# One decoder layer on one Trainium2 core: the FFN mean's factor moved in the order of the gate and up products, two weight sums moved to VectorE, one sum and one cast moved at the end

## The chip, the core and the metric

The kernel runs on 1 core of one Trainium2 chip. The core has a matrix engine (TensorE: PE, with its weight loads shown as PEld), three engines for everything else (VectorE: DVE; ScalarE: ACT; GpSimd: POOL), and SyncE (SP), which here issues most of the DMA transfers; POOL issues some too. The engines run side by side, each works through its own queue in order, and semaphores hold an instruction back until its inputs are there and its output buffer is free. Operands lie in SBUF (128 partitions); matmuls write PSUM, which has eight banks of 128 x 512 float32.

The metric is device time in microseconds (us) for one execution of the whole layer; lower is better. A profiled execution has besides a span, from its first to its last instruction.

## The reference

One layer of a hybrid decoder on 512 tokens of width 1024. It has a mixer (stick-breaking attention and a gated convolution), a cross-attention into 256 memory tokens, and a SwiGLU feed-forward part, each behind an RMS norm and followed by a residual add. The change is in the feed-forward part, cut here to what matters:

```python
def rms_norm(x, g):
    var = jnp.mean(xf * xf, axis=-1, keepdims=True)
    return xf * lax.rsqrt(var + EPS) * g
...
hf = rms_norm(x, norm_ffn[l])
gate, up = jnp.split(hf @ w_ffn_in[l], 2, axis=-1)        # 1024 x 2816 each
x = x + (jax.nn.silu(gate) * up) @ w_ffn_out[l]           # 2816 x 1024
```

The factor rsqrt(var + EPS) is one number per token. It can be multiplied in after the products, and the kernel does so.

## The kernel before

**Stages.** The mixer runs to about 346 us of the span, the cross-attention to about 502 us, the gate and up products to about 724 us, and the down projection with the final norm to the end. Activations are held transposed: features on partitions, tokens along the row. Every float32 operand is split into a rounded part (hi, cast by ACT) and a remainder (lo, a subtraction on DVE at L996 or alike), and each product is three matmuls: hi x hi, hi x lo, lo x hi.

**Gate and up products.** The 2816 hidden columns are 22 slices m of 128 (`NF` = 22). For a slice, gate and up over a pair of input blocks form a 2x2 block product, which is computed with seven products instead of eight (a Winograd form). So a slice needs seven products i = 0 to 6, each over four pairs of input blocks (`product`, L899). They add into three PSUM banks: `z` (i = 0, 3, 4, 5, one after the other), `v` (i = 1) and `y` (i = 2, then 6). After products 0, 3 and 4 ACT copies `z` away (`reads`, L935: tiles `sa`, `sb`); the next product into `z` cannot start before that copy is done. DVE adds the two halves of `v` after product 1 and of `y` after product 6 (L932 and L933), and of `y` once more before product 6 (`second`, L946); product 6 waits for the latter, because it overwrites the bank.

**Weights of a slice.** `ffn_load(m)` (L844) fetches two tiles, `wg` and `ws` (`s13`), with SP, and adds a third piece into `ws` with an accumulating transfer issued by POOL; `load_corner(m)` (L862) fetches `a`. Two sums then finish the seven weight combinations: `sum_third(m)` (L869) adds a half of `ws` into `wg`, and `sum_last(m)` (L873) writes the sum of the two halves of `wg` into `a`. Both are 128x512 additions, on DVE unless an engine is given. `pair_cast(m, which)` (L879) casts `wg`, `ws` or `a` (which = 0, 1, 2), 128x1024, on ACT for products (0, 1), (4, 2) or (5, 6); `third_cast(m)` (L896) casts the weight of product 3. `rest_of` (L995) takes the remainder on DVE. `made(n, cast, ...)` (L1112) queues the cast at place n and the remainder one place later.

**The order.** In this stage the program order of PE, ACT and DVE is written by hand (`manual_schedule`, L1184); SP and POOL, and all other stages, are laid out by a planner that works with the dependencies and estimated costs. The list `uses` (L970) gives the order of the products; n is a place in it:

```python
uses = [(0, 0), (0, 1), (0, 2), (1, 0), (1, 1), (0, 3), (1, 3), (0, 4), (1, 2), (0, 5), (0, 6),
        (1, 4), (2, 0), (2, 1), (1, 5), (1, 6)]
for m in range(2, NF - 1):
    uses += [(m, 3), (m, 2), (m, 4), (m + 1, 0), (m + 1, 1), (m, 5), (m, 6)]
```

so (1, 2) is place 8, and (0, 5), (0, 6) are places 9 and 10. At each n the loop at L1191 issues the product, then its reads, then what `at(n, ...)` has queued there, and last, at two values of n, the parts of the mean. For the last slices the list ends (20, 3), (20, 2), (20, 4), (21, 0), (21, 1), (20, 5), (21, 3), (21, 2), (21, 4), (20, 6), (21, 5), (21, 6). In the code at L1160, n is the place of (20, 5); from there on the first parts of the down projection are fitted in too: `w0` and `w1` are casts of its weights, `x0` to `x3` casts of its activations.

**The mean.** `mean2()` (`squares_mean`, L183) splits the sum of squares `acc` into `acch` and `accl` on DVE; `along` (L205) then multiplies both by a constant matrix on PE, which leaves the mean in the PSUM tile `varb`, and calls `rstd_of` (L118). That takes Ln and Exp on ACT for a first value, and refines it with one Newton step on DVE: `rv` = var + EPS, `ra` = y y, `ra` = -0.5 ra rv, `r0b` = (ra + 1.5) y. `turn_r2` (L980) writes a row of `r0b` to DRAM and reads it back turned, with two transfers of POOL. `evict` (L950) multiplies a slice by `r0b`, takes the SiLU on ACT, and forms the activation. `rstd_of` also serves the mixer's norm, the memory tokens' norm and the norm of the cross-attention.

Of the kernel before, what the change touches and what calls it, by code (L numbers as in the profile page):

```python
# [11 lines left out]
ALU = mybir.AluOpType  # L12
# [32 lines left out]
def hybrid_layer(ctx: ExitStack, tc: tile.TileContext, xT_d, memT_d, mem_d, cols_d, wv_d, win_d,  # L45
# [69 lines left out]
        after(i, [last])  # L115
        return [i]

    def rstd_of(var, n, s, tables=()):  # L118

        def new(t):  # L120
            return tmp(t, n) if n > TT else spool.tile([P, n], F32, tag=t, name=nm(t))

        v, y, a = new("rv"), new("ry"), new("ra")
        r = cpool.tile([P, n], F32, tag=s, name=nm(s))
        after(nc.scalar.activation(y, var, AF.Ln, bias=eps_t), tables)
        nc.vector.tensor_scalar(out=v, in0=var, scalar1=EPS, scalar2=None, op0=ALU.add)
        exps.append(nc.scalar.activation(y, y, AF.Exp, scale=-0.5))
        nc.vector.tensor_tensor(out=a, in0=y, in1=y, op=ALU.mult)
        nc.vector.scalar_tensor_tensor(out=a, in0=a, scalar=-0.5, in1=v, op0=ALU.mult,
                                       op1=ALU.mult)  # L130
        nc.vector.scalar_tensor_tensor(out=r, in0=a, scalar=1.5, in1=y, op0=ALU.add, op1=ALU.mult)
        return r

    def chained(i):

# [47 lines left out]
    def squares_mean(acc, n, folded=False):  # L183

        if folded:
            low, high = HALVES
            t, both = tmp("accf"), unit("acch", n * P)
            nc.scalar.copy(t[low, :], acc[high, :])
            nc.vector.tensor_tensor(out=t[low, :], in0=t[low, :], in1=acc[low, :], op=ALU.add)
            nc.vector.tensor_copy(both[low, :], t[low, :])  # L190
            nc.vector.tensor_tensor(out=both[high, :], in0=t[low, :], in1=f(both[low, :]),
                                    op=ALU.subtract)
            parts = both,
        else:
            parts = unit("acch", n * P), unit("accl", n * P)
            nc.vector.tensor_copy(parts[0], acc)
            nc.vector.tensor_tensor(out=parts[1], in0=acc, in1=f(parts[0]), op=ALU.subtract)

        def mean(bank):
            vp = bank("varb")[:, :n * P]  # L200
            for part in parts:
                nc.tensor.matmul(vp, mean_r, part, start=part is parts[0], stop=part is parts[-1])
            return vp

        def along(s, tables=(), bank=otile):  # L205

            vp = mean(bank)
            return rstd_of(vp, n * P, s, tables)

        def turned(s, tables=(), bank=otile):  # L210

            row = tmp("vrow")
            nc.scalar.copy(row[0:1, :n * P], mean(bank)[0:1, :])
            return rstd_of(turned_row(row[0:1, :n * P], n, "v" + s, nc.sync, nc.sync), n, s, tables)

        return along, turned


# [890 lines left out]
    def at(n, *some):  # L1109
        todo.setdefault(n, []).extend(some)  # L1110

    def made(n, cast, *args, late=1):  # L1112

        parts = []
        at(n, lambda: parts.append(cast(*args)))
        at(n + late, lambda: rest_of(*parts[0]))
# [3 lines left out]
    made(2, pair_cast, 0, 2)  # L1120
    at(3, lambda: load_corner(2))
    made(4, pair_cast, 1, 1)
    made(7, pair_cast, 2, 0)
    made(9, pair_cast, 1, 2)
    at(9, lambda: sum_third(2, nc.gpsimd))
    at(13, lambda: evict(0, 0))
    at(14, lambda: evict(0, 1))
    at(15, lambda: evict(0, 2))
# [2 lines left out]
    for m in range(1, NF - 1):  # L1131
        p = {i: uses.index((m, i)) for i in range(2, 7)}
        q = {i: uses.index((m + 1, i)) for i in range(2)}
        if m > 1:
            at(p[3], lambda m=m: sum_third(m + 1))
            at(p[3], lambda m=m: evict(m - 1, 0))
            at(p[2], lambda m=m: evict(m - 1, 1))
            at(q[0], lambda m=m: evict(m - 1, 2))
            made(p[3], pair_cast, m, 2)
            made(p[2], third_cast, m + 1)  # L1140
        else:
            made(p[4], third_cast, m + 1)
        at(p[4], lambda m=m: second(m))
        if m + 2 < NF:
            at(p[4], lambda m=m: load_corner(m + 2))
        made(q[0], pair_cast, m + 1, 1, late=2)
        at(q[1], lambda m=m: sum_last(m + 1)) if m > 1 else at(11, lambda: sum_last(2, nc.gpsimd))
        if m + 2 < NF:
            made(p[5], pair_cast, m + 2, 0)
    at(uses.index((0, 4)), lambda: second(0))  # L1150
# [7 lines left out]
        return lambda: rest_of(*held.pop(s))  # L1158

    n = uses.index((NF - 2, 5))  # L1160
    made(n, pair_cast, NF - 1, 2)
    at(n, lambda: begun("w0", out_cast, *w01(0))(), begun("x0", cast_first, 0))
    at(n + 1, ended("w0"), ended("x0"), begun("x2", half_form, 2, 0, 0))
    at(n + 2, ended("x2"), lambda: n2_of(halves(acts[0][1])[0], 0), begun("x1", cast_first, 1))
    at(n + 3, lambda: second(NF - 1), ended("x1"), begun("x3", half_form, 3, 0, 0), ended("x3"))
    at(n + 4, lambda: evict(NF - 2, 0), begun("x2", half_form, 2, 1, 0),
       lambda: begun("w1", out_cast, *w01(1))(), lambda: evict(NF - 2, 1), ended("x2"),
# [16 lines left out]
    with tc.manual_schedule(engines={mybir.EngineType.PE, mybir.EngineType.Activation,  # L1184
# [6 lines left out]
        for n, (m, i) in enumerate(uses):  # L1191
# [4 lines left out]
            reads(m, i)  # L1196
            for part in todo.get(n, ()):
                part()
            if n == 8:
                mean2 = mean2()  # L1200
            elif n == 10:
                r2b[0] = mean2[0]("r0b", bank=mmtile)
                turn_r2()

        evict(NF - 1, 1)
# [317 lines left out]
```

## Time and profile before

| what | us |
|---|---|
| time, median of 3 runs | 841.49 |
| lowest and highest run | 841.46 and 842.75 |
| the profiled execution, its time | 841.48 |
| the profiled execution, its span | 839.8 |
| gate and up products, from and to (of the span) | about 502 to 724 |
| busy in that window: PE, DVE, ACT, POOL | 221.13, 208.36, 116.26, 28.18 |

The profile is of one execution. A row of a timeline has the start in us from the span's start, the busy time in us, the engine, the line of the code, the operation, the tile written and the tiles read, shapes, and how many instructions are merged; brackets give the engine's idle time before it and what ended that. Matmuls overlap: their busy times add up to more than the distance of their starts. A row of the waits has the waiting engine, line and tile, what it waited for, and the total in us, the number of times and the longest.

### The profile page before, as it was taken

The numbers are of one execution on the slowest core, as the hardware profiler recorded it, in microseconds if no ns is written. First come the engines' busy times: TensorE is split into PE (matmuls) and PEld (weight loads), VectorE is DVE, ScalarE is ACT, GpSimd is POOL, SyncE is SP. The second block draws the span as 40 slices with busy tenths as digits, with TensorE's granted clock in tenths as the row PEclk, the third lists the DMA queues.
The fourth block names the chain that finished last, engine by engine and source line by source line (L and its number), as shares of the span: only waits on it lengthen the run. The fifth ranks groups of instructions, "written<-read, shape, count | busy, mean of one in ns | idle before, by whom it ended". The sixth has DMA issues, their size and how long they took to land.

```text
span 839.8 us, 12035 instructions
## 1 busy us (share of the span) xinstructions
PE 830.6 (99%) x4430; PEld 716.8 (85%) x4430; DVE 682.0 (81%) x1070; ACT 458.3 (55%) x778; POOL 164.2 (20%) x170
## 2 busy tenths in 40 slices
PE   9999999999999999999999999999999999999996
PEld 7888888888888888888888889999999999888885
DVE  7879899986756577586555689999999999999886
ACT  7567878674332355433444556644455545576654
POOL 0011131110666620173000032111111110000401
PEclk9999999999999999999999999999999999999999
DMA  8553454134687865556421326577767663465552
GB/s 302 153 167 101 121 115 112 61 121 167 235 314 274 314 230 199 188 229 235 151 75 51 101 65 161 152 180 198 200 170 204 179 181 96 165 216 197 178 184 101
DMA packets 51359, 143.70 MB, mean 171 GB/s; under 512 B 5762, under 2 KB 7042, under 8 KB 48483
## 3 DMA queue, kind: packets, MB, share of 16 engines
q1 hardware_dynamic: 41650, 107.89, 38.1%
q0 software_dynamic: 9360, 34.75, 15.6%
q8 instruction: 35, 0.57, 0.3%
q10 hardware_dynamic: 288, 0.28, 0.1%
q14 instruction: 26, 0.20, 0.1%
HBM read 125.20 MB, written 13.64 MB: 165 GB/s over the span
## 4 chain that ended last, share of the span: by engine, by line
PE 97%; DVE 1%; ACT 0%; issue 0%; DVEq 0%
PE z L911 14%; PE p L1216 12%; PE pr L156 8%; PE pr L158 8%; PE pr L157 8%; PE y L906 5%; PE r L157 3%; PE r L156 3%; PE r L158 3%; PE v L284 3%; PE v L906 2%; PE y L914 2%; PE km L662 2%; PE mq L158 2%; PE mq L156 2%; PE mq L157 2%
## 5 line engine op out<-in xcount | busy, mean ns | idle before, releaser
L151 ACT CAST wh<-wr 128x1024 fp32r<-128x1024 f32 x84 | 88.1, 1051 | 142.2 <-issue 75.3
L152 DVE TENSOR_TENSOR wl<-wr,wh 128x1024 fp32r<-128x1024 f32 x84 | 111.1, 1323 | 31.7 <-ACT wh L151 31.7
L156 PE MATMUL pr<-xgh,wh 128*128 128x512 f32 x288 | 112.8, 392 | 0.0
L157 PE MATMUL pr<-xgl,wh 128*128 128x512 f32 x288 | 112.3, 390 | 0.0
L158 PE MATMUL pr<-xgh,wl 128*128 128x512 f32 x288 | 112.2, 390 | 0.0
L607 POOL TENSOR_TENSOR pre<-pre 128x512 f32<-128x512 f32 x44 | 71.2, 1623 | 31.4 <-DMA pre<-in_w_ffn_out_dram 29.1
L859 POOL DMA_DIRECT2D ws<-in_w_ffn_in_dram x22 | 26.6, 1209 | 236.3 <-DVE c L704 53.9
L911 PE MATMUL z<-xdh,wf 128*128 128x256 f32 x352 | 70.0, 283 | 0.0
L158 PEld LDWEIGHTS pr<-xgh,wl 128*128 128x128 f32 x288 | 54.1, 188 | 11.6
L156 PEld LDWEIGHTS pr<-xgh,wh 128*128 128x128 f32 x288 | 54.1, 188 | 10.5
L157 PEld LDWEIGHTS pr<-xgl,wh 128*128 128x128 f32 x288 | 54.1, 188 | 10.5
L940 ACT COPY sa<-z 128x256 f32<-128x256 f32 x44 | 16.4, 373 | 78.9 <-PE z L911 76.7
L911 PEld LDWEIGHTS z<-xdh,wf 128*128 128x128 f32 x352 | 57.4, 190 | 0.1
L911 PE MATMUL z<-xdl,wf 128*128 128x256 f32 x176 | 49.7, 282 | 0.0
L996 DVE TENSOR_TENSOR wf<-wg,wf 128x1024 fp32r<-128x1024 f32 (+1 forms) x44 | 43.1, 979 | 1.6 <-ACT wf L884 0.2
L996 DVE TENSOR_TENSOR wl<-wr,wh 128x1024 fp32r<-128x1024 f32 x33 | 41.0, 1243 | 2.8 <-ACT wh L1063 2.8
L1063 ACT CAST wh<-wr 128x1024 fp32r<-128x1024 f32 x33 | 34.5, 1049 | 6.2 <-ACT f01h L992 2.6
L911 PE MATMUL z<-xf,wf 128*128 128x256 f32 x264 | 35.7, 283 | 0.0
L911 PE MATMUL z<-xc,wf 128*128 128x256 f32 x264 | 35.2, 283 | 0.2 <-ACT sa L940 0.2
L911 PEld LDWEIGHTS z<-xf,wf 128*128 128x128 f32 x264 | 33.4, 192 | 0.3 <-DVE wf L996 0.2
L911 PEld LDWEIGHTS z<-xc,wf 128*128 128x128 f32 x264 | 33.1, 190 | 0.5 <-ACT sa L940 0.4
L911 PEld LDWEIGHTS z<-xdl,wf 128*128 128x128 f32 x176 | 33.4, 190 | 0.0
(352 smaller groups left out, 2212.0 us busy)
## 6 DMA issues: line engine op xcount, KB each, us to landing
wr<-in_w_in_dram SPq DMA_DIRECT2D x36, 512.0 KB, 3.5
pre<-in_w_ffn_out_dram POOLq DMA_DIRECT2D x11, 1024.0 KB, 7.9
sums<-pre POOLq DMA_DIRECT2D x11, 1024.0 KB, 4.8
ws<-in_w_ffn_in_dram SPq DMA_DIRECT2D x22, 512.0 KB, 5.3
wg<-in_w_ffn_in_dram SPq DMA_DIRECT2D x22, 512.0 KB, 4.7
ws<-in_w_ffn_in_dram POOLq DMA_DIRECT2D x22, 512.0 KB, 5.8
wr<-sums SPq DMA_DIRECT2D x22, 512.0 KB, 3.9
wr<-in_w_ffn_out_dram SPq DMA_DIRECT2D x16, 512.0 KB, 4.0
```

Of the source, the lines that this page charges most:

```text
L151: after(nc.scalar.copy(h2, raw), lead[-1:])
L152: lows.append(nc.vector.tensor_tensor(out=l2, in0=raw, in1=f(h2), op=ALU.subtract))
L156: nc.tensor.matmul(ps, a[0], b[0], start=start, stop=False, **kw)
L157: nc.tensor.matmul(ps, a[0], b[1], start=False, stop=False, **kw)
L158: nc.tensor.matmul(ps, a[1], b[0], start=False, stop=stop, **kw)
L607: nc.gpsimd.tensor_tensor(out=t[:, a, :], in0=t[:, a, :], in1=t[:, b, :], op=ALU.add)
L859: nc.gpsimd.dma_start(s13, a[:, 0:4:3, :], accum_op=ALU.add)
L906: nc.tensor.matmul(ps, hi, both[0], start=i < 3 and k == 0, stop=False, skip_group_check=True)
L911: nc.tensor.matmul(ps[:, :HS], a, b, start=i < 3 and k == 0 and j == 0, stop=k == KP - 1 and j == 2, skip_group_check=True)
L996: nc.vector.tensor_tensor(out=lo, in0=src, in1=f(hi), op=ALU.subtract)
L1063: nc.scalar.copy(hi, raw)
L1216: nc.tensor.matmul(res[i][s2], a[:, ts], b, start=j == 0 and n == 0, stop=n == 2 and j == (BEHIND - 1 if (i, s2) == (5, 1) else NJ - 1))
```

## The change

- `rstd_of` loses the tile `rv` and its addition. The Newton step becomes three operations: `a` = -0.5 y y, then `a` = (var + EPS) a, reading `var` where it lies, then (a + 1.5) y as before. With `later=True` it returns these three as a function to be called afterwards, and `along` passes that on.
- The mean of the feed-forward norm: `mean2()` is called after place 6 instead of 8; the mean's matmuls, Ln and Exp come after place 8 instead of 10; the three DVE operations and `turn_r2` come after place 9 instead of 10.
- `pair_cast(2, 0)` is queued at place 6 instead of 7.
- `sum_third(2)` runs on DVE at place 10 (before: on POOL, queued at 9), and `sum_last(2)` on DVE at place 13, that of (2, 1) (before: on POOL, queued at 11).
- At the end, `sum_last(21)` is queued after (20, 4) instead of (21, 1), `pair_cast(21, 2)` at (21, 1) instead of (20, 5), and the cast of `x0` and its remainder one place later each; `w0` stays.

```diff
--- before.py
+++ after.py
@@ -115,21 +115,26 @@
         after(i, [last])
         return [i]
 
-    def rstd_of(var, n, s, tables=()):
+    def rstd_of(var, n, s, tables=(), later=False):
 
         def new(t):
             return tmp(t, n) if n > TT else spool.tile([P, n], F32, tag=t, name=nm(t))
 
-        v, y, a = new("rv"), new("ry"), new("ra")
+        y, a = new("ry"), new("ra")
         r = cpool.tile([P, n], F32, tag=s, name=nm(s))
         after(nc.scalar.activation(y, var, AF.Ln, bias=eps_t), tables)
-        nc.vector.tensor_scalar(out=v, in0=var, scalar1=EPS, scalar2=None, op0=ALU.add)
         exps.append(nc.scalar.activation(y, y, AF.Exp, scale=-0.5))
-        nc.vector.tensor_tensor(out=a, in0=y, in1=y, op=ALU.mult)
-        nc.vector.scalar_tensor_tensor(out=a, in0=a, scalar=-0.5, in1=v, op0=ALU.mult,
-                                       op1=ALU.mult)
-        nc.vector.scalar_tensor_tensor(out=r, in0=a, scalar=1.5, in1=y, op0=ALU.add, op1=ALU.mult)
-        return r
+
+        def refined():
+            nc.vector.scalar_tensor_tensor(out=a, in0=y, scalar=-0.5, in1=y, op0=ALU.mult,
+                                           op1=ALU.mult)
+            nc.vector.scalar_tensor_tensor(out=a, in0=var, scalar=EPS, in1=a, op0=ALU.add,
+                                           op1=ALU.mult)
+            nc.vector.scalar_tensor_tensor(out=r, in0=a, scalar=1.5, in1=y, op0=ALU.add,
+                                           op1=ALU.mult)
+            return r
+
+        return refined if later else refined()
 
     def chained(i):
 
@@ -202,10 +207,9 @@
                 nc.tensor.matmul(vp, mean_r, part, start=part is parts[0], stop=part is parts[-1])
             return vp
 
-        def along(s, tables=(), bank=otile):
-
-            vp = mean(bank)
-            return rstd_of(vp, n * P, s, tables)
+        def along(s, tables=(), bank=otile, later=False):
+
+            return rstd_of(mean(bank), n * P, s, tables, later)
 
         def turned(s, tables=(), bank=otile):
 
@@ -1120,9 +1124,9 @@
     made(2, pair_cast, 0, 2)
     at(3, lambda: load_corner(2))
     made(4, pair_cast, 1, 1)
-    made(7, pair_cast, 2, 0)
+    made(6, pair_cast, 2, 0)
     made(9, pair_cast, 1, 2)
-    at(9, lambda: sum_third(2, nc.gpsimd))
+    at(10, lambda: sum_third(2))
     at(13, lambda: evict(0, 0))
     at(14, lambda: evict(0, 1))
     at(15, lambda: evict(0, 2))
@@ -1144,7 +1148,7 @@
         if m + 2 < NF:
             at(p[4], lambda m=m: load_corner(m + 2))
         made(q[0], pair_cast, m + 1, 1, late=2)
-        at(q[1], lambda m=m: sum_last(m + 1)) if m > 1 else at(11, lambda: sum_last(2, nc.gpsimd))
+        at(q[1] if m < NF - 2 else p[4], lambda m=m: sum_last(m + 1))
         if m + 2 < NF:
             made(p[5], pair_cast, m + 2, 0)
     at(uses.index((0, 4)), lambda: second(0))
@@ -1158,10 +1162,10 @@
         return lambda: rest_of(*held.pop(s))
 
     n = uses.index((NF - 2, 5))
-    made(n, pair_cast, NF - 1, 2)
-    at(n, lambda: begun("w0", out_cast, *w01(0))(), begun("x0", cast_first, 0))
-    at(n + 1, ended("w0"), ended("x0"), begun("x2", half_form, 2, 0, 0))
-    at(n + 2, ended("x2"), lambda: n2_of(halves(acts[0][1])[0], 0), begun("x1", cast_first, 1))
+    made(n - 1, pair_cast, NF - 1, 2)
+    at(n, lambda: begun("w0", out_cast, *w01(0))())
+    at(n + 1, ended("w0"), begun("x0", cast_first, 0), begun("x2", half_form, 2, 0, 0))
+    at(n + 2, ended("x0"), ended("x2"), lambda: n2_of(halves(acts[0][1])[0], 0), begun("x1", cast_first, 1))
     at(n + 3, lambda: second(NF - 1), ended("x1"), begun("x3", half_form, 3, 0, 0), ended("x3"))
     at(n + 4, lambda: evict(NF - 2, 0), begun("x2", half_form, 2, 1, 0),
        lambda: begun("w1", out_cast, *w01(1))(), lambda: evict(NF - 2, 1), ended("x2"),
@@ -1196,10 +1200,12 @@
             reads(m, i)
             for part in todo.get(n, ()):
                 part()
-            if n == 8:
+            if n == 6:
                 mean2 = mean2()
-            elif n == 10:
-                r2b[0] = mean2[0]("r0b", bank=mmtile)
+            elif n == 8:
+                mean2 = mean2[0]("r0b", bank=mmtile, later=True)
+            elif n == 9:
+                r2b[0] = mean2()
                 turn_r2()
 
         evict(NF - 1, 1)
```

## The prediction

> **What bounds the kernel now.** I read the page's busy times first, then the list of waits for PE alone, then the timelines of PE, DVE, ACT and POOL around each wait found there.
>
> ```profile
> span 839.8 us, 12035 instructions
> PE 830.6 (99%) x4430; PEld 716.8 (85%) x4430; DVE 682.0 (81%) x1070; ACT 458.3 (55%) x778; POOL 164.2 (20%) x170
> ```
>
> PE works 830.6 of 839.8 us. Nothing in the diff removes a matmul, so it can give back only time in which PE stands or runs thin. The list of PE's waits over the whole run shows where:
>
> ```profile
> PE warm L244 <- DVE neg L92: 1.4, 1, 1.4
> PE y L906 <- DVE sb L933: 0.4, 1, 0.4
> PE z L911 <- ACT sa L940: 0.2, 1, 0.2
> PE varb L202 <- DVE accl L197: 0.2, 1, 0.2
> ```
>
> The first belongs to the start and is untouched. The other three all lie in the gate and up products, and each ends on an instruction that the diff moves or unburdens. Idle time undercounts such a wait, because PE also loses some time as it drains and starts again. So I take starts, and compare the disturbed blocks with the same blocks in an undisturbed slice. First the front of the stage; a product takes one row, or several rows where operands alternate:
>
> ```profile
> 515.38 0.28 PE L911 MATMUL z<-xdh,wf 128*128 128x256 f32 x1
> ...
> 518.21 0.40 PE L202 MATMUL varb<-acch,mean_r 128*128 128x512 f32 x1
> 518.85 0.50 PE L202 MATMUL varb<-accl,mean_r 128*128 128x512 f32 x1 [0.24 <-DVE accl L197]
> 519.19 1.59 PE L911 MATMUL z<-xc,wf 128*128 128x256 f32 x12
> ...
> 524.77 0.28 PE L911 MATMUL z<-xdh,wf 128*128 128x256 f32 x1
> 525.43 1.21 PE L906 MATMUL y<-xo,wf 128*128 128x512 f32 x4 [0.38 <-DVE sb L933]
> ...
> 526.96 0.28 PE L911 MATMUL z<-xdh,wf 128*128 128x256 f32 x1
> ...
> 531.22 1.84 PE L911 MATMUL z<-xf,wf 128*128 128x256 f32 x12
> 532.89 1.09 PE L906 MATMUL v<-xo,wf 128*128 128x512 f32 x4
> ```
>
> Then an undisturbed slice and, below it, the end of the stage:
>
> ```profile
> 704.77 0.28 PE L911 MATMUL z<-xdh,wf 128*128 128x256 f32 x1
> ...
> 706.30 0.28 PE L911 MATMUL z<-xdh,wf 128*128 128x256 f32 x1
> ...
> 707.73 1.09 PE L906 MATMUL y<-xc,wf 128*128 128x512 f32 x4
> ...
> 710.56 1.60 PE L911 MATMUL z<-xf,wf 128*128 128x256 f32 x12
> 712.00 1.09 PE L906 MATMUL v<-xo,wf 128*128 128x512 f32 x4
> ...
> 716.26 1.09 PE L906 MATMUL y<-xc,wf 128*128 128x512 f32 x4
> ...
> 718.07 1.69 PE L911 MATMUL z<-xc,wf 128*128 128x256 f32 x12 [0.24 <-ACT sa L940]
> 719.60 1.09 PE L906 MATMUL y<-xo,wf 128*128 128x512 f32 x4
> ```
>
> An undisturbed pair of mean matmuls is in the chain of waits, at the earlier mean of the same shape:
>
> ```profile
> 396.00 0.48 PE varb L202 x2
> ```
>
> Four losses follow. The mean's pair: 519.19 - 518.21 = 0.98, less 0.48, is **0.50**. Product (1,6), from the last matmul of (1,5) to the next product: 526.96 - 524.77 = 2.19, against 706.30 - 704.77 = 1.53, is **0.66**. Product (3,0): 532.89 - 531.22 = 1.67, against 712.00 - 710.56 = 1.44, is **0.23**. The end, a y and a z block: 719.60 - 716.26 = 3.34, against 710.56 - 707.73 = 2.83, is **0.51**. Together 1.90 us.
>
> **The change part by part.** Why DVE is late at the first three:
>
> ```profile
> 512.08 1.22 DVE L996 TENSOR_TENSOR wf<-ws,wf 128x1024 fp32r<-128x1024 f32 x1
> ...
> 517.13 1.67 DVE L197 TENSOR_TENSOR accl<-acc,acch 128x512 fp32r<-128x512 f32 x1
> ...
> 519.50 2.43 DVE L996 TENSOR_TENSOR wf<-a,wf 128x1024 fp32r<-128x1024 f32 x1
> 521.85 0.68 DVE L126 TENSOR_SCALAR rv<-varb 128x512 f32<-128x512 f32 x1
> ...
> 523.89 0.69 DVE L131 SCALAR_TENSOR_TENSOR r0b<-ra,ry 128x512 f32<-128x512 f32 x1
> 524.50 0.42 DVE L932 TENSOR_TENSOR sb<-y,sb 128x256 f32<-128x256 f32 x1
> ...
> 530.34 1.22 DVE L996 TENSOR_TENSOR wf<-wg,wf 128x1024 fp32r<-128x1024 f32 x1
> ```
>
> At the earlier mean the same subtraction took 0.69, and POOL ran its two sums just over the two long ones here:
>
> ```profile
> 393.58 0.69 DVE L197 TENSOR_TENSOR accl<-acc,acch 128x512 fp32r<-128x512 f32 x1
> ```
>
> ```profile
> 516.85 1.39 POOL L871 TENSOR_TENSOR wg<-ws,wg 128x512 f32<-128x512 f32 x1 [9.60 <-DVE wf L996]
> ...
> 519.09 1.75 POOL L875 TENSOR_TENSOR a<-wg 128x512 f32<-128x512 f32 x1
> ```
>
> **The two sums** (`sum_third(2)`, `sum_last(2)`) go to DVE. That adds two 128x512 operations, about 2 x 0.69 = 1.38 us by the accl row, and takes away (1.67 - 0.69) + (2.43 - 1.22) = 2.19 us of stretching. DVE gains 0.81, and the larger part comes ahead of the mean, while the added sums run after the factor is done. The Trainium skill (Perfetto Trace Analysis, Optimizing Scalar/DVE Operations) says that a saturated DVE may be relieved by handing work to GPSIMD, which speaks against this edit, and adds that the port the two share may spoil it. What the first half of that rule would make of the time is the third rival below.
>
> **The mean's parts sooner** (`mean2()` at n = 6 instead of 8, its matmuls at 8 instead of 10). DVE is free at 512.08 + 1.22 = 513.30; the cast and the subtraction, at no more than 0.69 each, end by 514.7. The pair now stands ahead of the product at 515.38, so it has 0.7 us to spare and the 0.50 goes. The ACT rows give the rest:
>
> ```profile
> 512.74 0.37 ACT L940 COPY sa<-z 128x256 f32<-128x256 f32 x1 [1.07 <-PE z L911]
> ...
> 519.39 0.69 ACT L125 ACTIVATE ry<-varb,eps_t 128x512 f32<-128x512 f32 x1 [2.95 <-PE varb L202]
> 520.11 0.63 ACT L127 ACTIVATE ry<-ry 128x512 f32<-128x512 f32 x1
> ```
>
> Ln starts 0.20 after the pair is through (519.39 - 519.19), so at 515.38 + 0.48 + 0.20 = 516.06; Exp ends 0.72 + 0.63 later, at 517.4. While ACT waits for Ln, `pair_cast(1,2)` (n = 9) stands behind it and runs to 518.5 at latest; its remainder is wanted by product (1,5), which starts about 523 (524.77 + 0.12 less a z block of 1.44 and the 0.50), so this added wait hides unless it grows by several us. `pair_cast(2,0)` moves one use up, behind the copy at 512.74; at 1.05 us (a cast of this size, in the rows of the end) it is done by 512.74 + 0.37 + 1.05 = 514.2. The z copy behind it is then done by 514.6, ahead of product (0,5) at 515.38 + 0.48 = 515.9. On DVE the cast's remainder (1.22) and `second(0)` (2 x 0.42) follow the mean's parts, from 514.7 to 516.8; product (0,6), which overwrites that bank, now starts at 515.9 + 1.44 = 517.3. Slack 0.5, the shortest cover of the front: without it PE waits there, inside the mean's gain.
>
> **Three operations** instead of four. The add on `rv` (0.68) ran while ACT was long done, so here it sat on DVE's path. What remains is three dependent operations, 0.68 from start to start ((523.89 - 521.85) / 3), now from 517.4 to 517.4 + 2 x 0.68 + 0.69 = 519.5; r0b was ready at 523.89 + 0.69 = 524.6. The middle one reads PSUM, as the L126 row did at 0.68, so I price it like the rest. In the three other uses of `rstd_of` the add goes too, where PE has no wait to give back: nothing gained. POOL's two small transfers for `rt` follow r0b and come 5 us sooner; nothing before the last stage reads them, and the accumulating loads queued behind them only gain.
>
> **What is late next.** From 519.5 DVE has a joined pair (2 x 0.42), the remainder of `pair_cast(1,2)` (1.22), `sum_third(2)` (0.69) and `second(1)` (2 x 0.42): done at 523.1. PE wants the y bank for (1,6) at 525.43 - 0.54 - 0.50 = 524.4 (0.54 is 525.43 - 524.77 less one undisturbed 0.12). Slack 1.3, so the 0.66 goes. Product (3,0) suffered because its remainder ended at 530.34 + 1.22 = 531.56. `second(1)` ended about 525.4 and now 523.1; less the added `sum_last(2)`, everything behind comes 1.6 sooner, at 530.0, while PE arrives at 531.22 - 1.16 = 530.06 and reads that remainder in its third matmul. This is the least sure term, its cover nearly nil: 0.23 if it holds, 0 if not, and up to 0.3 more from the blocks behind it, which are thin in the same way.
>
> **The end.** Here ACT works down a queue before it can copy the z bank:
>
> ```profile
> 715.23 1.05 ACT L884 CAST wf<-a 128x1024 fp32r<-128x1024 f32 x1 [1.65 <-issue]
> ...
> 717.66 0.36 ACT L940 COPY sa<-z 128x256 f32<-128x256 f32 x1
> ```
>
> Before 715.23 ACT idles 1.65 us for the last sum. With `sum_last(21)` two uses sooner, `pair_cast(21,2)` fills that idle time, `w0`'s cast follows and `x0`'s moves behind the copy. The cast and `w0`, 2 x 1.05 from the 713.6 where ACT fell idle (715.23 - 1.65), end near 715.7. The sum has to be done by 713.6, 1.6 sooner than ACT saw it, and two uses are 2.8 (707.73 to 710.56). The copy then runs as soon as product (21,3) is through, at 716.3 instead of 717.66. The 0.51 goes. DVE's amount of work here is unchanged, and `x0`'s parts are wanted only by the next stage, four products on.
>
> Sum: 841.48 (the profiled execution, 1.68 around its span of 839.8, and 0.01 from the median of 841.49) less 1.90 is **839.6 us**, or 0.23% less. If the thin blocks recover too: 839.3.
>
> **The rivals.** *One stretch keeps its wait.* The copy at the end may still stand behind a cast that waits for a buffer, or (3,0) may stay thin. For it: DVE's cover there is under 0.2 us. Against: the end's buffers belonged to products two uses back. Time: 839.8 with (3,0) alone, 840.1 with the end alone, 840.3 with both.
>
> *The order elsewhere shifts.* `rstd_of` also serves three means outside the part ordered by hand; without `rv` the planner may lay out DVE, SP and POOL anew. PE has no wait there now, so this can only cost: one 1.22 remainder out of its place makes 839.6 + 1.2 = 840.8.
>
> *DVE is the bound* (the slower side). In the stage's window DVE is nearly as full as PE:
>
> ```profile
> 502.00:724.00 222.00, 221.13 (x1591) 208.36 (x1590) 208.36 (x350) 116.26 (x190) 28.18 (x25) 1.00 0.64 171
> ```
>
> The columns are length, then busy time of PE, PEld, DVE, ACT and POOL, granted clock and DMA: DVE works 208.36 of 222 us, 94%. If the long operations are long for another reason than POOL, the sums cost 1.38 less 0.68 for `rv`, DVE reaches (3,0)'s remainder at 531.56 + 0.70 = 532.3, and PE, there at 530.1, waits 2.2: 839.6 + 0.23 + 2.2 = 842.0. It decides once that remainder ends after 530.3. Against it stand 0.69 and 1.67 for one shape without and with POOL at work. The Trainium skill (SBUF — State Buffer, Who interferes with whom) has a DVE operation with two SBUF inputs wait out a GPSIMD one that reads SBUF; by that rule accl would end 0.69 after 516.85 + 1.39, at 518.93, and the trace has 518.80.
>
> *It gives nothing*: PE's ends are modelled, and the waits could be too. But 0.64 lies between the starts of the mean's two matmuls, and starts are recorded. Time 841.5.
>
> **How the numbers follow.** Forecast 0.60; one stretch 0.18; order elsewhere 0.12; DVE bound 0.06; nothing 0.04. About 0.2% (1.68 us, so 839.8) is what a measurement of this kernel can tell from no change, and the forecast clears it by 0.2 only. I count four fifths of the forecast (0.48) as faster and 0.01 of the rest; slower by 0.2% means over 843.2, beyond every price above, 0.04 for a DVE backlog larger than priced or two shifts elsewhere; 0.47 within. The range runs from 839.2 (all thin blocks recovered and a little) to 840.9, which takes in the first two rivals.
>
> **What would show it.** Right: no PE wait on accl, on the `sb` join or on `sa` at the end; accl at 0.69 and r0b five us before 524.6; the copy at the end about 716 less the front's gain. Wrong: a PE wait at (0,5) or (0,6) because the moved cast holds ACT or DVE; the remainder of (3,0) still after its product starts; a new PE wait before 500 us.

## The result and the profile after

The changed kernel took 839.72 us, the median of 10 runs (839.23 to 840.45), against 841.73 for the kernel before beside it (841.39 to 842.75). The ratio is 0.9976, with a 95% interval from 0.9967 to 0.9984. That is the side that was forecast (839.6, range 839.2 to 840.9). The bound of 0.2% is cleared by the ratio and not by the whole of its interval. The profiled execution took 839.23 us.

First the page's busy times of the kernel after, then its list of PE's waits over the whole run:

```profile
span 837.5 us, 12030 instructions
PE 829.3 (99%) x4430; PEld 717.1 (86%) x4430; DVE 683.1 (82%) x1068; ACT 459.2 (55%) x778; POOL 163.9 (20%) x168
```

```profile
PE warm L248 <- DVE neg L92: 1.4, 1, 1.4
```

The number of matmuls is the same, and of the four waits only the one at the start is left. The timeline of PE has the same places as before (start, busy time, instruction; the line numbers moved by a few):

```profile
515.29 0.40 PE L207 MATMUL varb<-acch,mean_r 128*128 128x512 f32 x1
515.53 0.39 PE L207 MATMUL varb<-accl,mean_r 128*128 128x512 f32 x1
515.76 0.28 PE L915 MATMUL z<-xdh,wf 128*128 128x256 f32 x1
...
524.17 0.28 PE L915 MATMUL z<-xdh,wf 128*128 128x256 f32 x1
524.29 1.09 PE L910 MATMUL y<-xo,wf 128*128 128x512 f32 x4
...
525.69 0.28 PE L915 MATMUL z<-xdh,wf 128*128 128x256 f32 x1
...
529.96 1.60 PE L915 MATMUL z<-xf,wf 128*128 128x256 f32 x12
531.40 1.09 PE L910 MATMUL v<-xo,wf 128*128 128x512 f32 x4
...
714.57 1.11 PE L910 MATMUL y<-xc,wf 128*128 128x512 f32 x4
...
717.42 1.09 PE L910 MATMUL y<-xo,wf 128*128 128x512 f32 x4
```

Start to start, the mean's pair now takes 515.76 - 515.29 = 0.47 (0.98 before), product (1,6) 525.69 - 524.17 = 1.52 (2.19), product (3,0) 531.40 - 529.96 = 1.44 (1.67), and the two blocks of the end 717.42 - 714.57 = 2.85 (3.34). All four are within 0.02 of the undisturbed values that the prediction took them to.

DVE and ACT over the same places:

```profile
513.58 0.69 DVE L202 TENSOR_TENSOR accl<-acc,acch 128x512 fp32r<-128x512 f32 x1
...
515.77 0.42 DVE L937 TENSOR_TENSOR sb<-y,sb 128x256 f32<-128x256 f32 x1
517.34 0.69 DVE L129 SCALAR_TENSOR_TENSOR ra<-ry 128x512 f32<-128x512 f32 x1 [1.14 <-ACT ry L126]
...
518.79 0.69 DVE L133 SCALAR_TENSOR_TENSOR r0b<-ra,ry 128x512 f32<-128x512 f32 x1
...
522.38 0.42 DVE L937 TENSOR_TENSOR sb<-y,sb 128x256 f32<-128x256 f32 x1
...
528.36 1.22 DVE L1000 TENSOR_TENSOR wf<-wg,wf 128x1024 fp32r<-128x1024 f32 x1
```

```profile
515.96 0.69 ACT L125 ACTIVATE ry<-varb,eps_t 128x512 f32<-128x512 f32 x1 [1.50 <-PE varb L207]
...
714.77 0.37 ACT L944 COPY sa<-z 128x256 f32<-128x256 f32 x1 [0.98 <-PE z L915]
```

Two idle times in brackets matter. DVE now stands 1.14 us before the Newton step, waiting for Exp. In the kernel before it never stood there, because it came to the step later than ACT did. And ACT stands 0.98 us before the copy at the end, which now waits for PE; before, PE waited for the copy.

**One yardstick for all runs.** The moment at which the stage starts differs between profiled executions by up to 0.8 us (502.50 after, 503.34 in one experiment). So I measure the stage alone, from the first z matmul of the gate and up products to the first p matmul of the next stage: 502.58 to 723.83 before, **221.25**; 502.50 to 721.65 after, **219.15**. The difference of 2.10 is nearly the whole of the spans' difference (839.8 - 837.5 = 2.3). To see where a kernel loses, each matmul's start, counted from the stage's first, is set against the start of its like in the kernel after; the steps of that difference are the losses. "Cover" compares DVE with PE at product (3,0): the start of that product, plus 0.24 for the two matmuls ahead of the one that reads the remainder, less the remainder's end. After: 529.96 + 0.24 - (528.36 + 1.22) = 0.62. The column (2,5) is the product that PE comes to after (3,0) and (3,1).

| kernel | median us | ratio to before, 95% interval | stage us | mean | (1,6) | (3,0) | (2,5) | end | cover at (3,0) |
|---|---|---|---|---|---|---|---|---|---|
| before | 841.73 | | 221.25 | 0.52 | 0.66 | 0.23 | 0.19 | 0.49 | -0.10 |
| after | 839.72 | 0.9967 to 0.9984 | 219.15 | 0 | 0 | 0 | 0 | 0 | 0.62 |
| three operations alone | 841.10 | 0.9986 to 1.0005 | 220.58 | 0.51 | 0 | 0.26 | 0.18 | 0.48 | -0.10 |
| sums on DVE alone | 841.26 | 0.9986 to 1.0005 | 220.93 | 0.01 | 0.25 | 0.86 | 0.18 | 0.48 | -0.71 |
| mean sooner alone | 840.07 | 0.9970 to 0.9989 | 219.65 | 0 | 0 | 0 | 0 | 0.49 | 1.13 |
| end alone | 841.36 | 0.9984 to 1.0003 | 220.94 | 0.52 | 0.84 | 0.26 | 0.18 | 0 | -0.11 |
| after, mean late | 840.49 | 0.9971 to 0.9990 | 219.85 | 0.01 | 0 | 0.51 | 0.18 | 0 | -0.37 |
| after, sums on POOL | 839.69 | 0.9963 to 0.9983 | 219.15 | 0 | 0 | 0 | 0 | 0 | 1.14 |
| after, four operations | 839.47 | 0.9955 to 0.9981 | 219.15 | 0 | 0 | 0 | 0 | 0 | 0.60 |
| after, old end | 840.41 | 0.9971 to 0.9989 | 219.65 | 0 | 0 | 0 | 0 | 0.50 | 0.60 |
| two of the four parts | 839.40 | 0.9964 to 0.9982 | 219.15 | 0 | 0 | 0 | 0 | 0 | 1.13 |
| after, two more on DVE | 840.90 | 0.9979 to 0.9998 | 220.20 | 0 | 0 | 0.86 | 0.19 | 0 | -0.70 |

Each ratio is to runs of the kernel before on the same chip, with medians from 841.67 to 841.98. The medians follow the stage within a few tenths; the stage says where. The intervals of three operations alone, sums alone and end alone take in 1, so what each of these parts is worth rests on the stage of one profiled execution, not on the medians. One run of the memset's kernel described below took 2953.25 us against 839.28 to 840.07 for its seven others, and is left out of its time.

### The profile page after: what moved, and what is told of

Its sections match the earlier page's. It is cut to its first block, busy times and chain, and to the rows that moved or that the text cites. A ratio compares the mean times of both kernels' runs of the same rounds, so it can differ in the third digit from the quotient of the medians.

```text
span 837.5 us, 12030 instructions
## 1 busy us (share of the span) xinstructions
PE 829.3 (99%) x4430; PEld 717.1 (86%) x4430; DVE 683.1 (82%) x1068; ACT 459.2 (55%) x778; POOL 163.9 (20%) x168
## 4 chain that ended last, share of the span: by engine, by line
PE 99%; DVE 0%; ACT 0%; DVEq 0%; issue 0%
PE z L915 15%; PE p L1222 12%; PE pr L161 8%; PE pr L162 8%; PE pr L163 8%; PE y L910 5%; PE r L162 3%; PE r L161 3%; PE r L163 3%; PE v L288 3%; PE y L918 2%; PE v L910 2%; PE km L666 2%; PE mq L163 2%; PE mq L161 2%; PE mq L162 2%
## 5 line engine op out<-in xcount | busy, mean ns | idle before, releaser
L157 DVE TENSOR_TENSOR wl<-wr,wh 128x1024 fp32r<-128x1024 f32 x84 | 113.2, 1348 | 32.1 <-ACT wh L156 32.0
L611 POOL TENSOR_TENSOR pre<-pre 128x512 f32<-128x512 f32 x44 | 73.8, 1681 | 33.6 <-DMA pre<-in_w_ffn_out_dram 31.3
L1000 DVE TENSOR_TENSOR wl<-wr,wh 128x1024 fp32r<-128x1024 f32 x33 | 41.0, 1243 | 3.3 <-ACT wh L1067 3.3
```

What stands on the lines that cost most here:

```text
L157: lows.append(nc.vector.tensor_tensor(out=l2, in0=raw, in1=f(h2), op=ALU.subtract))
L611: nc.gpsimd.tensor_tensor(out=t[:, a, :], in0=t[:, a, :], in1=t[:, b, :], op=ALU.add)
L1000: nc.vector.tensor_tensor(out=lo, in0=src, in1=f(hi), op=ALU.subtract)
```

## The experiments

**Theory and rivals.** My theory was the prediction's: the front's three losses are one lateness of DVE, and each part takes some of it away. What was open was which part does the work. One rival made the two sums the cure, since they had stretched two long DVE operations; another made the shorter Newton step the cure. So each part was first put alone into the kernel before, and then taken alone out of the kernel after.

**Three operations alone.** Only `rstd_of` is changed.

```diff
-        nc.vector.tensor_scalar(out=v, in0=var, scalar1=EPS, scalar2=None, op0=ALU.add)
...
-        nc.vector.tensor_tensor(out=a, in0=y, in1=y, op=ALU.mult)
-        nc.vector.scalar_tensor_tensor(out=a, in0=a, scalar=-0.5, in1=v, op0=ALU.mult,
-                                       op1=ALU.mult)
+        nc.vector.scalar_tensor_tensor(out=a, in0=y, scalar=-0.5, in1=y, op0=ALU.mult,
+                                       op1=ALU.mult)
+        nc.vector.scalar_tensor_tensor(out=a, in0=var, scalar=EPS, in1=a, op0=ALU.add,
+                                       op1=ALU.mult)
```

> Kernel before with the three-operation Newton step alone; the mean stays late, the sums stay on POOL. Stage length = start of the first gate product to start of the first down-projection matmul: 221.25 us before, 219.15 after. Theory (DVE's queue is the path from the mean to second(1), so any 128x512 operation taken out of it brings the y join forward by its 0.60 us start to start): the wait ahead of product (1,6) shrinks by about 0.6, the mean's own 0.50 and the end's 0.51 stay, (3,0) stays as late as before because DVE and PE both move: stage 220.6 to 220.8. Rival (the add on rv is hidden beside ACT's Ln and Exp, as it is at the mixer's mean): stage 221.25, nothing gained.

Measured: the stage is 220.58 (the range began at 220.6), 0.67 shorter, and the whole of that is the loss at (1,6). PE's timeline there and at (3,0):

```profile
525.38 1.09 PE L911 MATMUL y<-xo,wf 128*128 128x512 f32 x4
...
531.05 1.84 PE L916 MATMUL z<-xf,wf 128*128 128x256 f32 x12
532.73 1.09 PE L911 MATMUL v<-xo,wf 128*128 128x512 f32 x4
```

The block at 525.38 is back to 1.09 busy, without a releaser. Product (3,0) still takes 532.73 - 531.05 = 1.68. So on its own the dropped addition did lie on DVE's path, as the prediction said.

**Sums on DVE alone.**

```diff
-    at(9, lambda: sum_third(2, nc.gpsimd))
+    at(10, lambda: sum_third(2))
...
-        at(q[1], lambda m=m: sum_last(m + 1)) if m > 1 else at(11, lambda: sum_last(2, nc.gpsimd))
+        at(q[1], lambda m=m: sum_last(m + 1))
```

> Kernel before with the two sums of slice 2 on DVE alone. Theory (POOL's sums stretch DVE's accl and the remainder behind it, but DVE must then do the sums itself and has no idle time up to (3,0)): accl 0.69 and wf 1.22, the mean's 0.50 goes, the wait at (1,6) shrinks only a little (second(1) about 0.6 earlier, PE 0.5 earlier), and (3,0) gets later by what PE has gained, since its remainder is ready no sooner: 0.23 grows to about 0.9. Stage 220.9 to 221.3, nearly nothing gained. Rival (each loss is tied to the operation that was stretched, so DVE's net 0.81 removes the mean's wait and most of the wait at (1,6)): stage 220.0 to 220.3.

Measured: 220.93, a gain of 0.32. DVE's timeline, then PE's at product (3,0):

```profile
517.60 0.69 DVE L197 TENSOR_TENSOR accl<-acc,acch 128x512 fp32r<-128x512 f32 x1
...
519.69 1.22 DVE L996 TENSOR_TENSOR wf<-a,wf 128x1024 fp32r<-128x1024 f32 x1
...
530.51 1.22 DVE L996 TENSOR_TENSOR wf<-wg,wf 128x1024 fp32r<-128x1024 f32 x1
```

```profile
530.78 0.40 PE L911 MATMUL z<-xf,wf 128*128 128x256 f32 x2
531.78 1.46 PE L911 MATMUL z<-xf,wf 128*128 128x256 f32 x10 [0.60 <-DVE wf L996]
```

The stretch is gone (0.69 and 1.22 for 1.67 and 2.43), and with it the mean's 0.51 and 0.41 of product (1,6). But 0.63 of that comes back at (3,0). Counted from the stage's start, PE arrives there 0.92 sooner than before (530.78 - 503.06 = 27.72, against 28.64), while DVE, with two sums of 0.68 and 0.69 on it, ends the remainder only about 0.3 sooner (531.73 - 503.06 = 28.67, against 28.98). The expected stage was met, and the rival that made the sums the cure fell. A remainder late at (3,0) is also what the prediction's slower rival had, at a higher price and on a condition that did not hold: the long operations were long for no other reason than POOL.

**Mean sooner alone**, with four operations, the sums on POOL and the old end; `pair_cast(2, 0)` goes with it; no run moves that cast apart from the mean.

```diff
-    made(7, pair_cast, 2, 0)
+    made(6, pair_cast, 2, 0)
...
-            if n == 8:
+            if n == 6:
                 mean2 = mean2()
-            elif n == 10:
-                r2b[0] = mean2[0]("r0b", bank=mmtile)
+            elif n == 8:
+                mean2 = mean2[0]("r0b", bank=mmtile, later=True)
+            elif n == 9:
+                r2b[0] = mean2()
                 turn_r2()
```

> Kernel before with only the mean's parts sooner (split after place 6, matmuls, Ln and Exp after 8, Newton step after 9, still four operations) and pair_cast(2,0) at 6; sums on POOL, end as before. Theory (what counts is that DVE waits for Exp in a stretch where it has nothing due, instead of doing the mean in front of second(1)): all losses of the front go, the end's 0.51 stays: stage 219.6 to 219.8. Rival (the stretching by POOL is the cause, and stays): POOL's sums then fall on the Newton step or on second(0), PE waits at (0,6) or (1,6): stage 220.2 or more.

Measured: 219.65, a gain of 1.60. PE's waits, besides the one at the start, are down to the end's, and POOL's two sums now fall where they hurt nobody (timelines of POOL and of DVE):

```profile
PE z L915 <- ACT sa L944: 0.2, 1, 0.2
```

```profile
516.00 1.29 POOL L875 TENSOR_TENSOR wg<-ws,wg 128x512 f32<-128x512 f32 x1 [8.38 <-DVE wf L1000]
517.37 1.30 POOL L879 TENSOR_TENSOR a<-wg 128x512 f32<-128x512 f32 x1
```

```profile
517.18 0.69 DVE L129 TENSOR_SCALAR rv<-varb 128x512 f32<-128x512 f32 x1 [0.47 <-ACT ry L125]
517.84 1.37 DVE L130 TENSOR_TENSOR ra<-ry 128x512 f32<-128x512 f32 x1
```

The subtraction for the mean is through before POOL starts. The one operation that is stretched (`ra`, 1.37) and the addition on `rv` come behind an idle time, and r0b still ends 17.67 into the stage, where it ended at 524.58 - 502.58 = 22.00 before.

**End alone.**

```diff
-        at(q[1], lambda m=m: sum_last(m + 1)) if m > 1 else at(11, lambda: sum_last(2, nc.gpsimd))
+        at(q[1] if m < NF - 2 else p[4], lambda m=m: sum_last(m + 1)) if m > 1 else at(11, lambda: sum_last(2, nc.gpsimd))
...
-    made(n, pair_cast, NF - 1, 2)
+    made(n - 1, pair_cast, NF - 1, 2)
```

and the three lines below it as in the change.

> Kernel before with the end alone: sum_last(21) after (20,4), pair_cast(21,2) at (21,1), the cast x0 one place later. Theory: the copy of z runs when (21,3) is through, the end's 0.51 goes and nothing else: stage 220.74. Rival (the copy then waits for something else, or the parts of x0 come too late for the down projection): stage 221.0 or more, or a new wait after 721 us.

Measured: 220.94 and not 220.74. The end itself lost nothing any more; the front lost 0.2 more than in the kernel before, whose order it shares. Its timelines of PE and DVE:

```profile
526.13 1.20 PE L906 MATMUL y<-xo,wf 128*128 128x512 f32 x4 [0.57 <-DVE sb L933]
```

```profile
520.01 2.62 DVE L996 TENSOR_TENSOR wf<-a,wf 128x1024 fp32r<-128x1024 f32 x1
```

POOL's second sum came 0.2 us later in this execution (16.70 into the stage, 16.50 before), and the stretched operation took 2.62 instead of 2.43. With the old front, then, one execution can lose 0.2 more than another, and a gain against the kernel before carries about that; the gain of the end is 0.49 by its own blocks.

The four gains add up to 0.67 + 0.32 + 1.60 + 0.49 = 3.08, and the whole change brings 2.10. The difference of 0.98 is well beyond those 0.2. The front's losses are shared: several parts can take away the same one.

**The kernel after, with one part taken out each.** First the mean's parts and `pair_cast(2, 0)` back at their old places (the diff of "mean sooner" backwards):

> Kernel after with the mean's parts and pair_cast(2,0) back at their old places (split after place 8, the rest after 10; cast at 7); three operations, sums on DVE and the end as after. Theory (DVE's queue between the late mean and product (3,0) holds more than PE leaves it time for): no wait at the mean or at (1,6), but the remainder of (3,0) comes about 0.8 us after PE arrives: stage 219.9 to 220.1 against 219.15. Rival (the three operations and the sums together give DVE the time, the place of the mean adds nothing): stage 219.15 to 219.3.

Measured: 219.85, a little under the range, with a wait at (3,0) in PE's timeline. The remainder ended 0.61 after PE arrived, and not 0.8:

```profile
531.09 1.46 PE L915 MATMUL z<-xf,wf 128*128 128x256 f32 x10 [0.27 <-DVE wf L1000]
```

The sums and the shorter step together cure the mean and (1,6), and leave (3,0) worse than before (0.51 against 0.23). Then the two sums back on POOL (the diff of "sums on DVE" backwards):

> Kernel after with the two sums of slice 2 back on POOL at their old places. Theory: with the mean sooner, POOL's sums fall beside second(0) and the wait for Exp, where DVE has time; they stretch one Newton operation at most by 0.7 and DVE saves the 1.2 us of doing them: stage 219.15, as after. Rival (moving the sums to DVE is what cures the stretch, as the prediction had it): a wait comes back, stage 219.4 or more.

Measured: 219.15, no loss. Timelines of POOL and of DVE:

```profile
517.71 1.30 POOL L879 TENSOR_TENSOR a<-wg 128x512 f32<-128x512 f32 x1
```

```profile
518.19 1.37 DVE L129 SCALAR_TENSOR_TENSOR ra<-ry 128x512 f32<-128x512 f32 x1 [1.14 <-ACT ry L126]
...
528.68 1.22 DVE L1000 TENSOR_TENSOR wf<-wg,wf 128x1024 fp32r<-128x1024 f32 x1
```

One operation is stretched by 0.68, and DVE is spared two sums; the cover at (3,0) is 1.14 instead of 0.62. Then the addition on `rv` back (four operations, called at the new place):

> Kernel after with four operations in the Newton step (rv again, in all four uses). Theory: DVE comes 0.60 later to the remainder of (3,0), so it ends at 530.2 where PE arrives at 530.0, and 0.1 to 0.2 is lost there: stage 219.2 to 219.4. Rival (the cover of 0.4 us that the profile shows behind it takes it all): stage 219.15.

Measured: 219.15; I had expected up to 0.25 more. The rival had the number but not the reason, for the cover is not used up (0.60 instead of 0.62). DVE's timeline:

```profile
517.17 0.69 DVE L129 TENSOR_SCALAR rv<-varb 128x512 f32<-128x512 f32 x1 [0.47 <-ACT ry L125]
...
519.29 0.69 DVE L133 SCALAR_TENSOR_TENSOR r0b<-ra,ry 128x512 f32<-128x512 f32 x1
```

The addition fills the time in which DVE waits for Exp. From the stage's start (502.99 here) r0b ends at 519.98 - 502.99 = 16.99, and in the kernel after at 519.48 - 502.50 = 16.98. Last, the old end:

> Kernel after with the end of before: sum_last(21) at (21,1), pair_cast(21,2) and x0 at (20,5). Theory: the end's wait of 0.5 comes back and nothing else: stage 219.66. Rival (with the front earlier DVE and ACT are ahead at the end too, so the wait is gone anyway): stage 219.15 to 219.3.

Measured: 219.65, and the same rows as in the kernel before, on PE and on ACT:

```profile
716.86 1.69 PE L915 MATMUL z<-xc,wf 128*128 128x256 f32 x12 [0.25 <-ACT sa L944]
```

```profile
714.01 1.05 ACT L888 CAST wf<-a 128x1024 fp32r<-128x1024 f32 x1 [1.65 <-issue]
...
716.44 0.36 ACT L944 COPY sa<-z 128x256 f32<-128x256 f32 x1
```

**What stretches a DVE operation.** Two kernels put one useless POOL operation (its result is not used) beside `accl` in the kernel after: an addition, or a one-column copy and a memset, which together read next to nothing.

```diff
+    def crowd():
+        lo, t = wforms[1, 4][1], f(unit("crowd"))
+        nc.gpsimd.tensor_tensor(out=t, in0=f(lo), in1=f(lo), op=ALU.add)
...
+            if n == 5:
+                crowd()
```

> The kernel after, with one added GpSimd addition of two 128 x 512 float32 SBUF tiles, whose result nothing uses, issued so that it runs beside the mean's remainder accl on VectorE. Theory (a GpSimd operation that reads SBUF holds up a VectorE operation with two SBUF inputs, as beside the sums of the kernel before, where accl took 1.67 us and not 0.69): accl takes 1.5 to 1.8 us, the remainder behind it and the second form of pair (0,3..) end about 1 us later, near 517.2, where TensorE wants them at 517.18; the products' stage is 219.15 to 219.35 us long. Rival (the stretch in the kernel before came from something else, such as the DMA traffic of that stretch): accl stays at 0.69 us and the stage at 219.15.

> As c_sum, but the added GpSimd work is a one-column copy and a memset of a 128 x 512 float32 tile, which reads nothing from SBUF. Theory (GpSimd's reads are what holds VectorE up): accl stays at 0.69 us, the stage at 219.15. Rival (any GpSimd operation holds VectorE up): accl takes 1.3 us or more.

The addition's kernel, on POOL and on DVE:

```profile
514.07 1.08 POOL L986 TENSOR_TENSOR crowd<-wf 128x512 f32<-128x512 f32 x1 [6.23 <-DVE wf L1004]
```

```profile
514.28 1.41 DVE L202 TENSOR_TENSOR accl<-acc,acch 128x512 fp32r<-128x512 f32 x1
```

The memset's kernel, on POOL and on DVE:

```profile
514.25 0.53 POOL L987 MEMSET crowd<- 128x512 f32 x1
```

```profile
514.18 0.69 DVE L202 TENSOR_TENSOR accl<-acc,acch 128x512 fp32r<-128x512 f32 x1
```

The addition doubles `accl` (1.41, a little below the 1.5 expected), and the memset leaves it alone, though it lies wholly beside it. The Trainium skill (SBUF — State Buffer, Who interferes with whom) says just this of DVE operations with two SBUF inputs: they contend with a GpSimd operation that reads SBUF, not with one that only writes. These rows agree. The stage stays at 219.15 in both (839.87 and 839.67 us): with the addition `second(0)` ended 0.73 later in stage time, which fitted into the cover of product (0,6).

**How much cover is left.** Two useless DVE additions ahead of the remainder for (3,0):

```diff
+            if n == 13:
+                u = f(unit("spare"))
+                for _ in range(2):
+                    nc.vector.tensor_tensor(out=u, in0=r2b[0], in1=r2b[0], op=ALU.add)
```

> The kernel after, with two added VectorE additions of 128 x 512 float32 tiles, whose result nothing uses, issued after the last sum of the front and ahead of the remainder that product (3,0) waits for. It measures how much cover that product has left. Theory (the remainder ends at 529.58 and TensorE comes to it at 529.96, so that 0.4 us is all): two operations of 0.6 to 0.69 us put the remainder at 530.8 to 531.0, and the idle time and the tail of the matmul behind it make the stage 219.8 to 220.0 us long. Rival (VectorE has idle time ahead of the remainder that takes the additions up): the stage stays at 219.15.

Measured: 220.20, more than the theory's 220.0. Timelines of DVE and of PE:

```profile
525.70 1.41 DVE L1206 TENSOR_TENSOR spare<-r0b 128x512 f32<-128x512 f32 x2
...
530.08 1.22 DVE L1000 TENSOR_TENSOR wf<-wg,wf 128x1024 fp32r<-128x1024 f32 x1
```

```profile
530.36 0.40 PE L915 MATMUL z<-xf,wf 128*128 128x256 f32 x2
531.36 1.45 PE L915 MATMUL z<-xf,wf 128*128 128x256 f32 x10 [0.59 <-DVE wf L1000]
```

In stage time the remainder is 1.34 later and the cover 0.62 becomes -0.70: nothing on DVE takes the additions up. The rival fell. The idle time of 0.59 costs 0.86 at the product, and 0.19 more is lost two products on, at (2,5), whose first two matmuls each come 0.1 later still. That second loss reaches PE by way of ACT. Timelines of ACT and of PE in this kernel, then of ACT in the kernel after:

```profile
532.66 0.63 ACT L960 ACTIVATE fg<-fg 128x512 f32<-128x512 f32 x1 [3.63 <-DVE fg L958]
...
533.71 0.37 ACT L944 COPY sb<-z 128x256 f32<-128x256 f32 x1
```

```profile
534.13 0.39 PE L915 MATMUL z<-xdh,wf 128*128 128x256 f32 x1
```

```profile
531.99 0.37 ACT L944 COPY sb<-z 128x256 f32<-128x256 f32 x1
```

Product (2,5) writes the bank that ACT copies to `sb` after product (2,4). In ACT's queue that copy stands behind the SiLU of an `evict`, whose input DVE makes (L958) right behind the late remainder and one sum. So the copy ends at 534.08, and the product starts at 534.13. The same 0.05 us lie between the two in all six kernels that lose time at (2,5); in the kernel after, the copy ends at 532.36, 0.44 ahead of the product (532.80).

**Two of the four parts**: the diffs of "mean sooner" and "end" together, on the kernel before.

> The kernel before with two of the four parts only: the mean's parts and pair_cast(2,0) sooner, and the end's order. The Newton step keeps its four operations and POOL keeps the two sums. Theory (every loss of the front goes with the mean's earlier place and that of the end with its order; the two other parts give nothing that is still to be had): the stage is 219.1 to 219.2 us, as in the kernel after, and the time 839.5 to 839.8. Rival (with four operations and stretched sums together the cover of a later product runs out, which no run with only one of them could show): a wait of 0.2 us or more at product (1,6) or (3,0) and a stage of 219.4 or more.

Measured: 219.15 and 839.40 us (11 runs; 839.5 was the least expected). DVE and PE at product (3,0):

```profile
528.02 1.22 DVE L1000 TENSOR_TENSOR wf<-wg,wf 128x1024 fp32r<-128x1024 f32 x1
```

```profile
530.13 1.60 PE L915 MATMUL z<-xf,wf 128*128 128x256 f32 x12
```

The remainder ends at 529.24, 0.9 us ahead of the product. Two parts give the whole gain. It is no faster than the kernel after, by intervals that overlap nearly wholly: PE's stage has nothing left that these edits could give back.

## Why the prediction was right, point by point

- **The mean's pair** (0.50): 0.52 was there and went. Ln was worked out for 516.06 and came at 515.96, r0b for 519.5 and ended at 519.48.
- **Product (1,6)** (0.66): 0.66. The slack was worked out as 1.3; the join that PE needs ended at 522.80, 1.5 before the product.
- **Product (3,0)** (0.23): it went, and this least sure term was safer than I wrote. I had the remainder at 530.0 and PE at 530.06; it was 529.58 and 529.96, and the product needs it 0.24 later still. Two more DVE operations, 1.34 together, overran that cover of 0.62. One would about fill it, and by my estimate from the same rows it would already cost time at (2,5), whose cover is 0.44 (not run).
- **The thin blocks behind** were the mis-sized term: I left them out of the sum as "up to 0.3 more", and 0.19 of it was real and went. They were also not "thin in the same way": the loss is at (2,5) alone, and PE waits there for ACT's copy, which DVE's lateness holds up. With it the five places make 0.52 + 0.66 + 0.23 + 0.19 + 0.49 = 2.09, against the 1.90 of the sum.
- **The end** (0.51): 0.49. The copy runs when product (21,3) is through, 714.77, as worked out, with ACT 0.98 ahead.
- **Product (0,6)**, "the shortest cover of the front" at 0.5: `second(0)` ended at 516.19 and PE came at 517.18, so it was 1.0. I had priced the cast and the subtraction at 0.69 each; the cast takes 0.42. Of the covers measured here, those of (2,5) and (3,0) are the shortest.
- **The two sums**: this is the reasoning that failed, without changing the time. "DVE gains 0.81" credited the sums with undoing the stretch. The working up to 530.0 at (3,0) did not use the 0.81: it charged both additions, 0.69 each, and took the long operations as short, so it came out right for another reason than the one given. The earlier mean alone moves the subtraction out of POOL's way, and what POOL then stretches lies next to DVE's idle time. With the sums on POOL, r0b comes 17.67 into the stage, 0.69 later than in the kernel after (16.98), yet the remainder for (3,0) ends sooner by 0.52. By the cover at (3,0), moving the sums costs half a microsecond of margin and buys nothing.
- **Three operations**: the prediction's reason (the addition sat on DVE's path because ACT was long done) was true of the kernel before, where it is worth 0.67. The same change's earlier mean makes DVE wait for Exp again, and then the addition is free. The prediction's own figures had this: `second(0)` done at 516.8 and Exp at 517.4 leave DVE 0.6 us idle, nearly the 0.68 of the addition. I worked out each part against the kernel before, and not against the other parts.
- **The rivals.** One stretch keeping its wait: none did. The order elsewhere: on SP and POOL nothing but the two sums differs, on ACT one activation of the mixer stands one place later, and outside the stage the spans differ by only 0.2. DVE as the bound: not here, and its condition was false, since `accl` took 0.69 with the sums off POOL. A late remainder at (3,0) is real all the same, 0.86 with the sums alone and 0.51 with the mean late; the 2.2 I gave it was too dear. Nothing at all: the stage is 2.10 shorter.

Left open: why the matmul behind a late one comes about 0.10 late again, as the second of (2,5) does. And no run takes the three edits of the end apart.

## What to carry to other kernels

When one engine's lateness shows at several places, work out each edit against the kernel with the other edits in it: single gains here added up to 3.08 where 2.10 was to be had, and a cured loss at one place brought 0.6 of it back at the next, where PE now came sooner. Move the chain that others wait for first; what contends with it may then fall into idle time, and the edits meant against the contention give nothing. Before adding work to a nearly full engine, list the cover at every later place where the bound engine meets it, not only at the one being cured, and also where it meets it through a third engine, as PE met DVE's lateness in ACT's copy at (2,5).

## What the runs showed of the hardware

A DVE operation held up by POOL ends a fixed time after POOL does. Five rows have the POOL operation's end, the DVE operation's end behind it, and the DVE operation's time alone. Before, `accl`: 518.24 and 518.80, so 0.56 behind, 0.69 alone. Before, `wf<-a`: 520.84 and 521.93, 1.09 behind, 1.22 alone. Sums back on POOL, `ra`: 519.01 and 519.56, 0.55 behind, 0.69 alone. The useless addition, `accl`: 515.15 and 515.69, 0.54 behind, 0.69 alone. Mean sooner alone, `ra`: 518.67 and 519.21, 0.54 behind, 0.69 alone. Each ends its own time less 0.13 to 0.15 after POOL, though POOL had between 0.82 and 1.34 left when it started: it does almost nothing until POOL is through.

And an idle time understates what a wait costs PE. Six places have the idle time of the profile and the loss from start to start: before, the mean 0.24 and 0.52, (1,6) 0.38 and 0.66, the end 0.24 and 0.49; and at (3,0) 0.27 and 0.51 (mean late), 0.59 and 0.86 (two more on DVE), 0.60 and 0.86 (sums alone). The loss is 0.24 to 0.28 larger each time. At the z matmuls the rows show where that lies. Each is listed as 0.28 busy, but the next matmul starts 0.12 behind it (524.17 and 524.29 in the kernel after), so an idle time counted from the listed end leaves out 0.16; and the matmul behind the late one comes about 0.10 later than it should. A loss can also have no idle time in the list of waits at all, like the 0.19 at (2,5).
